# A hybrid encoder trunk in fp32: the second wave of group B's projections copied into output tiles, its rotary parts beside the latents' products, the latents in another order, the last squares of the MLP tied to a later place

## The chip, the core and the metric

The kernel runs on one core of a Trainium2 chip. The metric is the device time of one execution in microseconds (us). TensorE is called PE in the profile, VectorE DVE, ScalarE ACT, GpSimd POOL, SyncE SP.

## What is computed

Two layers over x of 1024 tokens by 1024 features, float32. Each layer has a projection of the normed x whose columns go to four groups of heads, the groups' attentions, one output projection with the residual, and an MLP with squared ReLU:

```python
for l in range(DEPTH):                       # DEPTH = 2
    h = rms_norm(x, norm1_g[l])
    proj = h @ w_in[l]
    (a_cq, a_ckv, a_kr, b_q, b_k, b_v, c_q, c_k, c_v, d_q, d_k, d_v) = jnp.split(proj, splits, axis=-1)
    y_a = mla_mixer(a_cq, a_ckv, a_kr, ...)  # latents: q = norm(cq) @ w_uq, k, v = norm(ckv) @ w_uk, w_uv
    y_b = diff_mixer(b_q, b_k, b_v, ...)     # q, k rotary; two softmaxes, w = p0 - lam * p1
    y_c = swa_mixer(c_q, c_k, c_v, ...)      # window of 128, sinks
    y_d = na_mixer(d_q, d_k, d_v, na_rpb[l]) # neighbourhood on the 64-wide grid, with a bias
    mix = jnp.concatenate([rms_norm(y_a, ..), y_b, rms_norm(y_c, ..), rms_norm(y_d, ..)], axis=-1)
    x = x + mix @ w_out[l]
    h = rms_norm(x, norm2_g[l])
    x = x + jnp.square(jax.nn.relu(h @ w_up[l])) @ w_down[l]
return rms_norm(x, final_norm_g)
```

Group A has 4 heads over latents of 192 (query) and 128 (key and value), B 4 heads of two 32-wide parts, C 4 query heads, D 4 heads.

## The kernel before

The products are made of fp32r parts: `split` (L195, L198) writes the rounded high half on ACT, then the low half as a difference (`tt`, L189), for weights on POOL (wh, wl). Each product is three passes, high by high (L221), low by high (L222) and high by low (L223) as `passes` orders them. x and all activations stand with features on the partitions and tokens along the free axis.

The program is written in the order of the stages, and a scheduler decides the order of each engine's instructions from it, with a few hints in the code: `high_priority` draws work forward, and `issue_after(ins)` keeps what is inside it behind the instruction named.

**Group B.** The projections of B come in two waves of six PSUM banks (`several`, WAVES): per wave a tile of q, of k and of v. When a wave is done, ACT copies each bank raw into a tile (L480): at both waves into `ptile`, the ring of tiles named p (six of them) that the softmax uses for its scores and probabilities. From the raw copy an evacuation (`ev`, from `evacs_b`, L423 to L427) makes q and k rotary (part<-p,tabc: the cosine part; twice part<-p,tabs: the sine parts with halves exchanged; an addition; the split; the stores into qb and kb) or turns v. The first wave's additions and low halves stand on DVE, the second wave's on POOL (`self.eng`). The turning of v (`to_values`) makes four transposes into a bank: the first wave's are put off (`self.due`, drained by `catch_up` in later steps of a projection), the second's are done at once, in a bank "tr".

Then `weave` mixes attn_b (scores sb, L856; minimum of each row nm, L858 on DVE; exponentials on ACT; transposes tr, L892; products pv) with a fill: `proj_latent` (the latents' projections, mm<-xh) and then `proj_d` (the projections of D).

**The latents.** attn_d and, beside it, proj_c and `latent_up` (L740) follow. The latter loads the normed factors (rq, rkv: spread over the partitions), the latents (latp: high and low; the key's and value's latent, and the query's of 128 and of 64 rows, the latter loaded twice each) and multiplies them with w_lat: values, keys, then the query's parts and the query's rotary part. rkv is loaded first, rq last. The bias of D's heads comes through the same SP queue.

**The MLP.** mlp_up works in 16 groups with a scheme of seven products for each two by two block; its results (ev) are rectified (`relu2`, L1254: max(u, 0) times the norm's factor, on DVE; the square on ACT), their differences made (`differ`), and stored into acts. mlp_down runs j = 0 to 3, each with operations 1, 2, 6, 7, 4, 5 and 3, and adds each block into x (x<-u, x<-p on DVE, L189), on which the reuse of the bank u waits. raw are weights with their sums, far the rounded activations' low halves. Since the last group of mlp_up ends when mlp_down already begins, its end is kept as `finish_up`: two functions, of which mlp_down calls the first in j = 0 after the first operation, behind `rounded` (the last rounding of its operands), the second in j = 1. The p blocks of j = 0 are tied behind `self.rectified`, the rectification written last.

## Time and profile before

| | |
|---|---|
| median of 3 runs | 2660.11 us (2659.59 to 2661.64) |
| the profiled execution | 2666.08 us |
| its span, first to last instruction | 2664.3 us |
| granted clock of PE, mean | .971 |
| busy: PE, DVE, ACT, POOL | 2529.8 (95%), 1950.1 (73%), 1442.6 (54%), 1127.8 (42%) us |
| DMA | 385.00 MB, mean 145 GB/s |

Busy times are sums over the whole span and say how full an engine is on average. What a change at one place is worth is read there: by windows (busy time of every engine in a stretch), by the waits of an engine in it (which engine's instruction came last before it went on) and by the timeline of one engine. A timeline's row joins equal instructions that follow each other; in brackets stands the idle time before it and what ended it. The clock is granted in parts of the full 2.4 GHz: 1.00 or .50 for a stretch, between them where it changes in a window.

### The profile page before, as it was taken

Reading aid. Unit: us, or ns where it says so; the run is one execution under the profiler, and the core shown is the slowest. Engines: PE = TensorE matmul, PEld = TensorE weight load, DVE = VectorE, ACT = ScalarE, POOL = GpSimd, SP = SyncE. Lnnn points to the kernel's source line nnn. Section 1 sums busy time; section 2 is a strip of 40 time slices with the busy share of each in tenths; the row PEclk is TensorE's granted clock in tenths of the full one; section 3 lists DMA queues with packets and bytes.
Section 4 is the critical chain, followed back from the end, with each engine's and each line's share of the span. In section 5 each row is a group of like instructions: output and inputs, shape, how many; then the busy total and the mean of one; then the engine's idle time right before and its main releaser. Section 6 shows DMA issues by size and latency. Waiting matters only on the chain.

```text
span 2664.3 us, 37498 instructions
## 1 busy us (share of the span) xinstructions
PE 2529.8 (95%) x12320; PEld 2105.1 (79%) x12320; DVE 1950.1 (73%) x3403; ACT 1442.6 (54%) x2612; POOL 1127.8 (42%) x800
## 2 busy tenths in 40 slices
PE   8899988999999998999999999889999999999998
PEld 7678877887788886888877788777877888878886
DVE  6677767784986668887568777677849866688876
ACT  4577756663644444444436777666735444444445
POOL 2465633211055554454425656332011555555554
PEclk9889998999999999999998999989999999999999
DMA  5634598331244456444245445963221544664431
GB/s 167 181 89 127 145 266 252 106 92 36 76 162 150 152 189 240 145 140 143 93 120 150 117 134 145 291 199 90 84 71 32 187 154 150 228 215 149 129 119 64
DMA packets 191539, 385.00 MB, mean 145 GB/s; under 512 B 23712, under 2 KB 34928, under 8 KB 191344
## 3 DMA queue, kind: packets, MB, share of 16 engines
q1 hardware_dynamic: 176976, 356.90, 44.2%
q10 hardware_dynamic: 14368, 25.70, 2.8%
q8 instruction: 98, 1.61, 0.3%
q14 instruction: 97, 0.79, 0.1%
HBM read 261.20 MB, written 121.32 MB: 144 GB/s over the span
## 4 chain that ended last, share of the span: by engine, by line
PE 73%; DVE 11%; DMA 7%; ACT 4%; issue 3%; POOL 1%; SPq 1%; DVEq 0%; POOLq 0%; ACTq 0%
PE u L221 8%; PE u L223 8%; PE u L222 8%; PE mm L221 5%; PE p L223 5%; PE p L221 5%; PE p L222 5%; PE mm L222 5%; PE mm L223 5%; PE sb L856 3%; DVE p L858 3%; PE tr L892 2%; DVE part L189 2%; ACT p L861 1%; PE pv L881 1%
## 5 line engine op out<-in xcount | busy, mean ns | idle before, releaser
L189 POOL TENSOR_TENSOR wl<-raw,wh 128x512 fp32r<-128x512 f32 x424 | 605.6, 1430 | 698.9 <-ACT wh L195 675.0
L195 ACT ACTIVATE wh<-raw 128x512 fp32r<-128x512 f32 x448 | 281.3, 629 | 578.3 <-PE u L222 311.4
L189 POOL TENSOR_TENSOR wl<-ws,wh 128x512 fp32r<-128x512 f32 (+1 forms) x120 | 151.1, 1261 | 451.1 <-ACT wh L195 444.2
L221 PE MATMUL u<-far,wh 128*128 128x512 f32 x768 | 301.1, 392 | 11.4 <-DVE x L189 9.2
L223 PE MATMUL u<-far,wl 128*128 128x512 f32 x768 | 300.9, 392 | 6.7 <-POOL wl L189 6.7
L222 PE MATMUL u<-far,wh 128*128 128x512 f32 x768 | 300.7, 392 | 0.0
L189 DVE TENSOR_TENSOR raw<-raw 128x512 f32<-128x512 f32 x256 | 224.9, 886 | 79.4 <-DMA raw<-in_w_up 43.1
L189 DVE TENSOR_TENSOR ptl<-tr,pth 128x512 fp32r<-128x512 f32 (+2 forms) x384 | 237.8, 628 | 60.5 <-ACT pth L195 59.4
L861 ACT ACTIVATE p<-p,nm 128x1024 f32<-128x1024 f32 x192 | 220.1, 1147 | 79.0 <-DVE nm L858 77.2
L195 ACT ACTIVATE pth<-tr 128x512 fp32r<-128x512 f32 (+2 forms) x384 | 206.0, 547 | 99.7 <-PE tr L892 63.6
L223 PE MATMUL p<-far,wl 128*128 128x512 f32 (+1 forms) x648 | 251.0, 387 | 4.0 <-DVE wl L189 4.0
L221 PE MATMUL p<-far,wh 128*128 128x512 f32 (+1 forms) x648 | 251.3, 388 | 0.0
L222 PE MATMUL p<-far,wh 128*128 128x512 f32 (+1 forms) x648 | 250.9, 387 | 0.0
L856 PE MATMUL sb<-stack 96*128 96x512 f32 x640 | 223.2, 430 | 13.9 <-DVE nm L858 12.9
L189 DVE TENSOR_TENSOR far<-act,far 128x512 fp32r<-128x512 f32 x224 | 206.1, 949 | 14.6 <-ACT far L195 14.6
L189 POOL TENSOR_TENSOR p<-p 128x1024 f32<-128x1024 f32 x64 | 154.8, 2419 | 106.3 <-ACT p L944 99.5
L221 PEld LDWEIGHTS u<-far,wh 128*128 128x128 f32 x768 | 145.1, 189 | 43.3 <-issue 10.0
L223 PEld LDWEIGHTS u<-far,wl 128*128 128x128 f32 x768 | 145.3, 189 | 37.9 <-POOL wl L189 7.8
L222 PEld LDWEIGHTS u<-far,wh 128*128 128x128 f32 x768 | 145.2, 189 | 31.0 <-DVE far L189 0.8
L221 PE MATMUL mm<-xh,wh 128*128 128x512 f32 x416 | 166.8, 401 | 1.8 <-DVE part L189 1.6
L892 PE MATMUL tr<-ident,p 128*128 128x128 f32 x1024 | 162.1, 280 | 6.3 <-DVE ptl L189 5.4
L858 DVE CUSTOM_DVE_ANT_0 p<-sb,zero 128x512 f32<-128x512 f32 x192 | 129.3, 685 | 49.5 <-PE sb L856 22.1
(255 smaller groups left out, 6150.7 us busy)
## 6 DMA issues: line engine op xcount, KB each, us to landing
act<-acts SPq DMA_DIRECT2D x224, 256.0 KB
raw<-in_w_up SPq DMA_DIRECT2D x128, 256.0 KB
acts<-ev SPq DMA_DIRECT2D x128, 256.0 KB
raw<-in_w_down SPq DMA_DIRECT2D x128, 256.0 KB
acts<-ev ACTq DMA_DIRECT2D x96, 256.0 KB
ws<-in_w_in SPq DMA_DIRECT2D x76, 256.0 KB
rz<-drows SPq DMA_DIRECT2D x40, 256.0 KB
stack<-kd SPq DMA_DIRECT2D x32, 256.0 KB
```

The costliest lines, as they stand in the source:

```text
L189: return (eng or self.nc.vector).tensor_tensor(out=out, in0=a, in1=b, op=op)
L195: self.rounded = nc.scalar.activation(hi, src, AF.Copy)
L221: mm(ps, w[0], x[0][:, sl], start=start, stop=False)
L222: mm(ps, w[0], x[1][:, sl], start=False, stop=False)
L223: mm(ps, w[1], x[0][:, sl], start=False, stop=stop)
L856: self.nc.tensor.matmul(ps, q[:, qt * P:(qt + 1) * P], k[:, sl], start=i == 0, stop=i == len(passes) - 1)
L858: self.nc.vector.tensor_tensor_reduce(out=p[:, sl], in0=ps, in1=self.zero[:, 0:1].bitcast(F).broadcast_to([P, 512]), scale=-scale, scalar= ...
L861: self.nc.scalar.activation(p, p, AF.Exp, bias=nm[:, 1:2], scale=-1.0, accum_out=z)
L881: nc.tensor.matmul(out, v[:, kt], lo[:, sl], start=False, stop=kt == 7)
L892: nc.tensor.transpose(t[:, k * 256 + i * P:k * 256 + (i + 1) * P], p[:, (j * 2 + k) * P:(j * 2 + k + 1) * P], self.ident)
```

## The change

Three parts, each in both layers. First, the second wave's raw copies go into output tiles (`ypair`, the tiles named y), and its evacuations are queued and done one by one, each ahead of a step of proj_latent; its values are turned like the first wave's. Second, latent_up loads both factors first and then the query's latents ahead of the others, and multiplies in another order: query rotary, query 0, key 0, both values, query 1, key 1. Third, the end of the last group of mlp_up is divided anew: in j = 0 only one rectification and one addition are left (`free`), and the squares, the other two rectifications, the differences and their stores (`rest`) stand in j = 1, tied behind the last addition of its first operation. `self.rectified` is thereby the rectification in `free`.

```diff
         def evacs_b(t):
             return [self.ev_rope(tabs, qb[:, t]), self.ev_rope(tabs, kb[:, t]),
-                    self.ev_plain(rb, self.to_values(vb[2 * t:2 * t + 2], "tr" if t else "mm"))]
+                    self.ev_plain(rb, self.to_values(vb[2 * t:2 * t + 2]))]
...
+                    second = deque()
+
+                    def beside(steps):
+                        for s in steps:
+                            if second:
+                                ev, n, src = second.popleft()
+                                ev(n, src)
+                            yield s
+
                     for t in range(2):
                         for ev, b in zip(evacs_b(t), banks):
-                            raw = self.ptile()
+                            raw = self.ypair() if t else self.ptile()
                             for n in range(2):
                                 sl = slice(n * 512, n * 512 + 512)
                                 nc.scalar.activation(raw[:, sl], b[n], AF.Copy)
-                                ev(n, raw[:, sl])
+                                if t:
+                                    second.append((ev, n, raw[:, sl]))
+                                else:
+                                    ev(n, raw[:, sl])
...
-                    fill = chain(self.proj_latent(l, one, xs, rb, tabs, lat, krd, rows), proj_d())
+                    fill = chain(beside(self.proj_latent(l, one, xs, rb, tabs, lat, krd, rows)), proj_d())
...
     def latent_up(self, l, lat, rows, qa, ka, va):
-        rkv = self.big_tile(F, "rkv")
-        kv = latent(2, P)
-        self.spread(rkv, rows[1])
-        q = [latent(0, P), latent(1, 64)]
-        rq = self.big_tile(F, "rq")
-        self.spread(rq, rows[0])
+        rq, rkv = self.big_tile(F, "rq"), self.big_tile(F, "rkv")
+        self.spread(rq, rows[0])
+        self.spread(rkv, rows[1])
+        parts = []
+        for i, r in ((0, P), (1, 64), (2, P)):
...
+        w0 = self.weights(d["w_lat"][l, 0])
+        yield from two([w0[0], both(w0[1])], parts[0:2], self.ev_rope(tabs, qr))
         plain = lambda r, dst: self.ev_plain(r, self.to_parts(dst))
+        yield from two([w0[2], both(w0[3])], parts[0:2], plain(rq, qn[:, 0]))
+        w1 = self.weights(d["w_lat"][l, 1])
+        yield from two(w1[2:3], parts[2:3], plain(rkv, kn[:, 0]))
         w2 = self.weights(d["w_lat"][l, 2])
         for t in range(2):
-            yield from two(w2[t:t + 1], [kv], self.ev_plain(rkv, self.to_values(va[2 * t:2 * t + 2])))
-        w1 = self.weights(d["w_lat"][l, 1])
-        for t in range(2):
-            yield from two(w1[2 + t:3 + t], [kv], plain(rkv, kn[:, t]))
-        yield from two([w1[0], both(w1[1])], q, plain(rq, qn[:, 1]))
-        w0 = self.weights(d["w_lat"][l, 0])
-        yield from two([w0[0], both(w0[1])], q, self.ev_rope(tabs, qr))
-        yield from two([w0[2], both(w0[3])], q, plain(rq, qn[:, 0]))
+            yield from two(w2[t:t + 1], parts[2:3], self.ev_plain(rkv, self.to_values(va[2 * t:2 * t + 2])))
+        yield from two([w1[0], both(w1[1])], parts[0:2], plain(rq, qn[:, 1]))
+        yield from two(w1[3:4], parts[2:3], plain(rkv, kn[:, 1]))
...
-            self.finish_up = [lambda: (done4(s), done3(s)), lambda: differ(s)]
+            def free():
+                s.b21 = tmp()
+                rectify(s.b21, s.u, 0)
+                self.tt(s.u2, s.p, s.u2, ALU.add)
+
+            def rest():
+                nc.scalar.activation(s.b21, s.b21, AF.Square)
+                keep(s.q, 2, s.b21)
+                relu2(s.u3, s.u3, 1)
+                keep(s.q, 3, s.u3)
+                relu2(s.u2, s.u2, 1)
+                differ(s)
+
+            self.finish_up = [free, rest]
...
-                        add(m, 0, u[m])
+                        added = add(m, 0, u[m])
...
                 if j == 1:
-                    self.finish_up[1]()
+                    with tc.issue_after(added.ins):
+                        self.finish_up[1]()
```

What it moves, in three places. The first is DVE where layer 0's attn_b begins: sb are the scores, nm their minima, part<-p the rotary products of the second wave's raw copies; both<-mm, the turning of the first wave's values, is the last row that the two have in common. Before:

```order
L189 TENSOR_TENSOR both<-mm,both 128x8x64 x2
L189 TENSOR_TENSOR part<-p,tabc 128x512
L189 TENSOR_TENSOR part<-p,tabs 64x512 x2
L189 TENSOR_TENSOR part<-p,tabc 128x512
L858 ISA p,nm<-sb,zero 128x512
L858 ISA nm 128x1
L189 TENSOR_TENSOR part<-p,tabs 64x512 x2
L858 ISA p,nm<-sb,zero,nm 128x512
L858 ISA nm 128x1
L858 ISA p,nm<-sb,zero 128x512
L858 ISA nm 128x1
```

Now:

```order
L189 TENSOR_TENSOR both<-mm,both 128x8x64 x2
L867 ISA p,nm<-sb,zero 128x512
L867 ISA nm 128x1
L867 ISA p,nm<-sb,zero,nm 128x512
L867 ISA nm 128x1
L867 ISA p,nm<-sb,zero 128x512
L867 ISA nm 128x1
L867 ISA p,nm<-sb,zero,nm 128x512
L867 ISA nm 128x1
L867 ISA p,nm<-sb,zero 128x512
L867 ISA nm 128x1
L867 ISA p,nm<-sb,zero,nm 128x512
```

Behind the sixth reduction the rotary products follow, read from y (part<-y,tabc and part<-y,tabs), a few at a time between the following reductions.

The second place is DVE at the MLP's passage in layer 0; ev are the results of the last group of mlp_up, far and raw belong to j = 0 of mlp_down. Before:

```order
L189 TENSOR_TENSOR ev<-p,ev 128x512
L189 TENSOR_TENSOR far<-act,far 128x512 x8
L1256 SCALAR_TENSOR_TENSOR ev<-ev,rb 128x512
L1256 SCALAR_TENSOR_TENSOR ev<-u,rb 128x512
L189 TENSOR_TENSOR ev<-p,ev 128x512
L189 TENSOR_TENSOR far<-act,far 128x512
L1256 SCALAR_TENSOR_TENSOR ev<-ev,rb 128x512
L189 TENSOR_TENSOR raw<-raw 128x512 x4
L189 TENSOR_TENSOR far<-act,far 128x512 x3
L189 TENSOR_TENSOR raw<-raw 128x512
L189 TENSOR_TENSOR far<-act,far 128x512
```

Now:

```order
L189 TENSOR_TENSOR ev<-p,ev 128x512
L189 TENSOR_TENSOR far<-act,far 128x512 x8
L1270 SCALAR_TENSOR_TENSOR ev<-u,rb 128x512
L189 TENSOR_TENSOR raw<-raw 128x512 x4
L189 TENSOR_TENSOR ev<-p,ev 128x512
L189 TENSOR_TENSOR raw<-raw 128x512
L189 TENSOR_TENSOR far<-act,far 128x512
L189 TENSOR_TENSOR raw<-raw 128x512
L189 TENSOR_TENSOR far<-act,far 128x512
L189 TENSOR_TENSOR raw<-raw 128x512
L189 TENSOR_TENSOR far<-act,far 128x512
```

Two rectifications of ev are gone from here, and so are the four differences (ev<-ev) that stood between the additions into x that follow. They stand in j = 1, behind the last addition of the first operation:

```order
L189 TENSOR_TENSOR x_7190<-u,x_7190 128x512
L1270 SCALAR_TENSOR_TENSOR ev<-ev,rb 128x512 x2
L189 TENSOR_TENSOR far<-act,far 128x512 x2
L189 TENSOR_TENSOR raw<-raw 128x512
L189 TENSOR_TENSOR x_7169<-p,x_7169 128x512
L189 TENSOR_TENSOR ev<-ev 128x512
L189 TENSOR_TENSOR raw<-raw 128x512
L189 TENSOR_TENSOR x_7176<-p,x_7176 128x512
L189 TENSOR_TENSOR ev<-ev 128x512 x3
L189 TENSOR_TENSOR x_7183<-p,x_7183 128x512
```

The third place is SP's queue at the latents of layer 0. Before:

```order
L160 DMA rz<-drows 64x1024
L160 DMA v<-vd 128x1024
L160 DMA latp<-lat 128x1024 x2
L160 DMA rkv<-drows 128x1024
L160 DMA latp<-lat 128x1024 x2
L160 DMA latp<-lat 64x1024 x4
L160 DMA rq<-drows 128x1024
L160 DMA ws<-in_w_out 128x256
L160 DMA stack<-kd 64x1024 x2
L160 DMA stack<-kc 64x1024
L160 DMA bias<-in_bias 128x768
```

Now:

```order
L160 DMA rz<-drows 64x1024
L160 DMA rq<-drows 128x1024
L160 DMA rkv<-drows 128x1024
L160 DMA latp<-lat 128x1024 x2
L160 DMA latp<-lat 64x1024 x4
L160 DMA latp<-lat 128x1024 x2
L160 DMA bias<-in_bias 128x768
L160 DMA stack<-kd 64x1024 x2
L160 DMA stack<-qd 64x1024
```

The loads of the latents stand in one piece, with both factors ahead of them, and they come ahead of more of attn_d's loads (stack).

## Rows read from the trace of the kernel before

**Rows 1.** The page: the chain's shares by engine, and the group of GpSimd's low halves.

```profile
PE 73%; DVE 11%; DMA 7%; ACT 4%; issue 3%; POOL 1%; SPq 1%; DVEq 0%; POOLq 0%; ACTq 0%
...
L189 POOL TENSOR_TENSOR wl<-raw,wh 128x512 fp32r<-128x512 f32 x424 | 605.6, 1430 | 698.9 <-ACT wh L195 675.0
```

**Rows 2.** Windows, us: stretch, length, busy PE, PEld, DVE, ACT, POOL, PEclk, DMA share, GB/s.

```profile
98.00:118.00 20.00, 13.45 (x40) 9.04 (x39) 19.20 (x41) 13.95 (x24) 14.78 (x9) 0.58 0.51 153
118.00:155.00 37.00, 36.66 (x210) 31.58 (x209) 30.16 (x68) 28.42 (x46) 20.45 (x13) 1.00 0.43 124
155.00:180.00 25.00, 23.17 (x94) 17.50 (x93) 20.94 (x54) 18.64 (x30) 18.23 (x16) 0.66 0.40 117
1418.00:1438.00 20.00, 14.28 (x47) 10.16 (x46) 18.89 (x42) 14.73 (x24) 14.12 (x9) 0.66 0.58 175
```

**Rows 3.** Timeline of VectorE from 83 to 92 us: start, us, instruction.

```profile
83.53 0.69 DVE L189 TENSOR_TENSOR part<-p,tabc 128x512 f32<-128x512 f32 x1 [17.63 <-ACT p L480]
84.24 2.42 DVE L189 TENSOR_TENSOR part<-p,tabs 64x512 f32<-64x512 f32 x2
86.69 0.69 DVE L189 TENSOR_TENSOR part<-p,tabc 128x512 f32<-128x512 f32 x1
...
88.57 3.46 DVE L189 TENSOR_TENSOR part<-p,tabs 64x512 f32<-64x512 f32 x2 [0.58 <-POOL part L189]
```

**Rows 4.** Waits of TensorE, 98 to 120 us: total, times, longest.

```profile
PE sb L856 <- DVE nm L858: 5.3, 2, 2.9
```

**Rows 5.** Waits of TensorE, 1000 to 1060 us.

```profile
PE u L221 <- DVE x L189: 9.2, 2, 7.6
...
PE u L223 <- POOL wl L189: 0.6, 1, 0.6
```

**Rows 6.** Timeline of TensorE from 1054 to 1060.5 us.

```profile
1055.43 0.77 PE L221 MATMUL u<-far,wh 128*128 128x512 f32 x1 [7.58 <-DVE x L189]
...
1060.24 0.40 PE L223 MATMUL u<-far,wl 128*128 128x512 f32 x1
```

**Rows 7.** Timeline of VectorE from 1008 to 1060 us.

```profile
1012.94 1.77 DVE L1256 SCALAR_TENSOR_TENSOR ev<-ev,rb 128x512 f32<-128x512 f32 x1
...
1016.43 0.68 DVE L1256 SCALAR_TENSOR_TENSOR ev<-ev,rb 128x512 f32<-128x512 f32 x1
...
1032.77 0.68 DVE L189 TENSOR_TENSOR ev<-ev 128x512 f32<-128x512 f32 x1
...
1040.64 3.48 DVE L189 TENSOR_TENSOR ev<-ev 128x512 f32<-128x512 f32 x2
...
1048.73 1.75 DVE L189 TENSOR_TENSOR ev<-ev 128x512 f32<-128x512 f32 x1
...
1054.61 1.87 DVE L189 TENSOR_TENSOR x<-u,x 128x512 f32<-128x512 f32 x3
```

**Rows 8.** Timeline of TensorE from 2345 to 2350 us.

```profile
2347.67 0.79 PE L223 MATMUL u<-far,wl 128*128 128x512 f32 x1 [6.04 <-POOL wl L189]
```

**Rows 9.** The chain, 2335 to 2350 us, in order of time: start, us, what.

```profile
2340.29 7.34 POOL wl L189
```

**Rows 10.** Windows at the MLP's passage and in j = 1, layer 0.

```profile
1050.00:1060.00 10.00, 4.57 (x11) 3.68 (x12) 9.48 (x16) 0.00 (x0) 0.00 (x0) 0.50 0.77 257
1110.00:1120.00 10.00, 10.00 (x46) 8.29 (x45) 10.00 (x12) 4.31 (x8) 5.55 (x4) 1.00 0.30 93
1125.00:1130.00 5.00, 5.00 (x24) 4.14 (x23) 2.54 (x4) 1.26 (x2) 2.16 (x3) 1.00 0.83 260
```

**Rows 11.** Waits of TensorE, 350 to 490 us.

```profile
PE sb L1026 <- DVE nb L1102: 4.0, 1, 4.0
...
PE mm L221 <- DMA latp<-lat: 2.2, 1, 2.2
```

**Rows 12.** Window of the latents' loads.

```profile
350.00:372.00 22.00, 18.82 (x106) 16.08 (x104) 10.35 (x28) 12.65 (x34) 6.80 (x4) 1.00 1.03 305
```

**Rows 13.** Waits of VectorE, 340 to 490 us.

```profile
DVE p L1102 <- DMA bias<-in_bias: 12.7, 3, 7.0
```

More of the change, by code (lines that the diff above doesn't have):

```diff
@@ L741, in latent_up @@
         nc, d = self.nc, self.d
-        def latent(i, r):
+        rq, rkv = self.big_tile(F, "rq"), self.big_tile(F, "rkv")
[3 more added lines that the diff above has]
+        for i, r in ((0, P), (1, 64), (2, P)):
             p = []
@@ L748, in latent @@
                 p.append(t)
-            return tuple(p)
-        rkv = self.big_tile(F, "rkv")
-        kv = latent(2, P)
-        self.spread(rkv, rows[1])
-        q = [latent(0, P), latent(1, 64)]
-        rq = self.big_tile(F, "rq")
-        self.spread(rq, rows[0])
+            parts.append(tuple(p))
         tabs = self.table("32", rq, nc.gpsimd)
@@ L1254, in relu2, with rectify @@
             def relu2(v, src, n):
+                rectify(v, src, n)
+                nc.scalar.activation(v, v, AF.Square)
+                return v
+            def rectify(v, src, n):
                 self.rectified = nc.vector.scalar_tensor_tensor(out=v, in0=src, scalar=0.0, in1=rb[:, N[n]],
                                                                 op0=ALU.max, op1=ALU.mult)
-                nc.scalar.activation(v, v, AF.Square)
-                return v
             def keep(q, o, v, eng=None):
@@ L1449, in add @@
                 o = self.x[m][:, N[n]]
-                self.tt(o, ps, o, ALU.add)
+                return self.tt(o, ps, o, ALU.add)
             for j in range(4):
```

## The prediction

> **What bounds the kernel now.** I read the page's chain first: 73% of the end is TensorE, 11% VectorE, 7% DMA, 4% ScalarE [rows 1]. TensorE is busy for 2529.8 of 2664.3 us, so all that an order without a new instruction can win lies in some 134 us of TensorE's idle time, and in matmuls that run at half clock behind an idle stretch. So I looked where the change moves something, by windows, and asked in each what TensorE waits for. Three places come out, each once per layer (layer 1 is layer 0 plus about 1318 us).
>
> The first is the start of group B's attention. From 98 to 118 us VectorE is busy for 19.20 of 20 us and TensorE for 13.45, at a granted clock of .58; in layer 1 it is 18.89 and 14.28, at .66 [rows 2]. The waits of TensorE there name the softmax's minimum on VectorE (nm) first, 5.3 us [rows 4]: VectorE is the bound of that stretch, and its rotary work of the second wave stands in the same queue as the softmax. From 118 to 155, TensorE is full (36.66 of 37) and VectorE has 6.84 us free; from 155 to 180 TensorE loses 1.83 us [rows 2].
>
> The second is the loading of the latents, 350 to 400 us, where the DMA engines are full (share 1.03, 305 GB/s) [rows 12]. TensorE waits 2.2 us for a latent tile and 4.0 us for a softmax [rows 11], and VectorE 12.7 us in all for the band's bias, which is loaded through the same queue [rows 13].
>
> The third is the passage from the MLP's up to its down products. In layer 0 TensorE waits 9.2 us for VectorE's additions into x, 7.6 of it at once [rows 5, 6], and VectorE has no free time before that. In layer 1 it waits 6.04 us for a low half (wl) of GpSimd [rows 8], which took 7.34 us [rows 9] where the mean of 424 is 1.43 [rows 1].
>
> **The change, part by part.** No engine gets an instruction more or fewer; everything is order, so no term is a duration by itself, only what a queue holds when somebody waits for it.
>
> *The MLP's passage, layer 0.* Ahead of the three additions x<-u at 1054.61 that TensorE waits for, VectorE ran two rectifications and four differences that now stand in the next quarter (j = 1): 1.77, .68, .68, 3.48 for two, and 1.75, in all 8.36 us [rows 7]. At the .68 of an undisturbed one six would cost 4.1 us; the rest was sharing with GpSimd, which may move to whoever comes next. So VectorE arrives 4.1 to 8.4 us earlier. TensorE can win the wait of 9.2 at most, and with it part of the slow matmuls behind it: from 1055.43 to 1060.24 eleven matmuls start in 4.81 us, with the granted clock of that window at .50, the level of 1.2 GHz [rows 6, 10]; at 2.4 GHz they would take half, so 2.4 us hang on the wait. I take **-6 us**, about the middle of 4.1 and 8.4; bounds -1 (the sharing comes back, and more) and -10 (8.4 and most of the 2.4).
>
> *The same in layer 1.* There TensorE waits for GpSimd's wl. VectorE's work that goes away stands partly before, partly behind that wl, and what kept GpSimd out, the row of raw and far operations with two operands in SBUF, stays. The later b21 rectification reads PSUM and may let GpSimd in, or not. Bounds 0 and -8 (6.04 and some 2 of slow matmuls); nearest to an unchanged row, I take **-2**.
>
> *The work put into j = 1.* Two rectifications, four differences, three squares and six stores land behind the first block's last addition of j = 1. VectorE is full there (10.00 of 10 us from 1110 to 1120) but TensorE lost nothing, and by 1125 to 1130 VectorE is busy for 2.54 of 5 only [rows 10]. Six times .68 is 4.1 us against those 2.5 us of free time, and what TensorE has in hand there no row shows: 0 to 3 us of delay per layer; **+1** for both. ScalarE, which gets the squares and two of the stores, is busy for 4.31 of 10 us there [rows 10], so they hide. The tensors stored are read in j = 3 only. Four of the stores stand in SP's queue, now behind j = 1's twelve loads of activations; while they wait for the differences, the loads of weights for the second half of the quarter wait behind them. If the cover is gone, the products of operation 6 in j = 1 are late by what is left of the 4.1.
>
> *The second wave beside the latents.* The copies by ScalarE stay, into output tiles; so the second wave holds no tile of the p ring, which the softmax uses. Of VectorE's rotary work, .69, 2.42, .69 and 3.46, together 7.26 us, was done from 83.5 to 92 us [rows 3], while TensorE was full with the wave's last products and the first latents. In the new order VectorE goes straight into six score reductions there, and those 7.26 us fall later. The second reduction can stand some 4 us earlier, since nothing of 3.46 us is ahead of it. The price has two ends: a loss of 7.26 per layer if they fall into VectorE's full stretch, a gain of up to 6.55 us (5.72 in layer 1), TensorE's idle time of it, if the softmax goes ahead and the rotary work moves to where TensorE has products. The only free VectorE time beside such products is the 6.84 us of 118 to 155, about what is moved. So I take **0** per layer, bounds -7 and +7. The two transposes of values that were done at once are now queued, at the same cost.
>
> *The latents in their old order.* First rq and rkv are loaded (1.05 MB), then all latent tiles, the query's first. The first product needs two tiles more (1.05 MB), its second half another two. At 305 GB/s [rows 12] 3.1 MB take 10.3 us, where before 1.05 MB (3.4 us) let the first product go. Against it: all loads stand together and earlier in SP's queue, ahead of head 1's bias, whereas rq came last before. The bounds per layer are +7 (10.3 - 3.4, in full) and -6 (the waits of 2.2 and 4.0 gone [rows 11]); in between, the nearest row is the wait of 2.2, a change of which is small: **0**. That the bias comes later falls to VectorE's waits for it, 12.7 us over three, of which TensorE felt at most 4.0.
>
> The sum: -6 - 2 + 1 + 0 + 0 = **-7 us** against the profiled execution of 2666.08, so 2659.1. That execution is 5.97 above the median of the runs, 2660.11, so in the terms of the runs the forecast is **2653.0 us**. The bounds of the three terms of the MLP alone reach from -18 to +5.
>
> **A rule against it.** GpSimd's low half took 7.34 us in layer 1 while VectorE ran operations on SBUF back to back, and a pair of VectorE's rotary operations 3.46 us [rows 3, 9]. The Trainium skill, "SBUF — State Buffer", section "SBUF: two separate sides", says that VectorE's operations with two SBUF operands and GpSimd's share a port pair that is an exclusive lock: who starts first has it for the whole instruction, the other stops. The trace agrees with the stop, by 7.34 against 1.43. In both orders 14 operations on SBUF alone stand ahead of the first addition into x; by that rule they can keep GpSimd out in layer 0 as in layer 1, and the sum would be -2 in place of -7.
>
> **The rivals.**
> - *GpSimd is locked out at both passages.* Layer 0 exchanges the wait of 9.2 for one like layer 1's 6.04, with the same slow matmuls behind; that is -3; layer 1 gives 0, j = 1 +1: -2, or **2658 us**. For it: the 7.34 us. Against it: in layer 0 TensorE waits for wl only 0.6 us [rows 5].
> - *The interleaving fills TensorE.* The stretches of 98 to 118 lose 6.55 and 5.72 us; if the softmax's head start carries through, both layers win that: 2653 - 12.3, about **2640 us**. For it: VectorE full and named by the waits [rows 2, 4]. Against it: the work is the same and comes in a full stretch.
> - *Slower: VectorE's early time is lost.* The 7.26 us of rotary work that TensorE covered from 83 to 92 now fall where VectorE sets the pace, in both layers: 2653 + 14.5, about **2667 us**. It decides above 6.2 us per layer ((5.3 + 7)/2). For it: VectorE is idle for 17.63 us before 83.5 [rows 3] and full behind 98. Against it: its 6.84 us free from 118 on.
> - *The latents stand at their loads.* At +6 per layer: 2653 + 12, **2665 us**. For it: full DMA engines; against it: the earlier issue.
> - That the change doesn't do what it says is excluded by the order of the instructions: the rotary work, the loads and the differences stand where the diff says.
>
> **How the numbers follow.** A measurement of this kernel can tell 0.2% (5.3 us) from no change, so faster is below 2654.8, slower above 2665.4. Forecast .36 (.33 faster, .03 same; by itself 2647 to 2658), filling .20 (faster), early time lost .17 (slower), lock .15 (same), loads .12 (.09 same, .03 slower): faster .53, same .27, slower .20. The range goes from the filling's 2641 to 2666, by the lost time's edge; left out are the ends on both sides, some .2.
>
> **What would show it.** Right: TensorE's wait for x from 1000 to 1060 us falls from 9.2 to about 3, the windows of 98 to 118 keep about 13.5 us of TensorE, and no wait for latp above 5 us appears. Wrong: a wait for wl of 6 us in both layers (the lock), TensorE above 17 us from 98 to 118 (filling) or a longer stretch of its half clock (lost time), a wait for latp near 7 us (loads).

## The result, and the profile after

The changed kernel takes 2672.47 us (median of 6 runs, 2668.89 to 2677.04) against 2658.05 for the kernel before in 6 runs beside it: a ratio of 1.0056, 95% interval 1.0041 to 1.0071. It is **slower by some 15 us**, where 7 us less were forecast. It lies outside the range, on the side and some 5 us beyond the size of the third rival (VectorE's early time lost, 2667).

A word on the reference of all that follows. The kernel before ran 71 times in five sets beside the others, 2652.3 to 2671.7 with medians of 2658 to 2661, but its two profiled executions took 2666.08 and 2667.54. The profile that the prediction read is thus an execution 6 us above the median. Where one profile of the attention in its old order is needed, I therefore also use that of experiment e3 (below), which leaves the attention as it was and whose profiled execution, 2652.6, is its own median.

Windows of the changed kernel at the start of layer 0's attention, in the columns of [rows 2]:

```profile
80.00:92.00 12.00, 12.00 (x54) 9.88 (x53) 2.21 (x7) 4.09 (x8) 2.59 (x2) 1.00 0.96 241
98.00:118.00 20.00, 13.59 (x62) 10.53 (x60) 15.63 (x31) 11.25 (x18) 13.47 (x7) 0.91 0.30 90
118.00:155.00 37.00, 34.54 (x178) 29.11 (x179) 33.59 (x69) 23.99 (x40) 26.46 (x18) 0.92 0.50 134
155.00:180.00 25.00, 19.25 (x90) 14.94 (x89) 19.58 (x54) 19.26 (x32) 16.91 (x15) 0.79 0.49 153
```

and of the kernel before in the first of them:

```profile
80.00:92.00 12.00, 12.00 (x54) 9.90 (x53) 7.82 (x8) 4.72 (x9) 6.05 (x4) 1.00 1.03 228
```

From 80 to 92 us VectorE is now busy for 2.21 us where it was for 7.82: the rotary work is gone from there. From 98 to 118 it is busy for 15.63 of 20 (19.20 before). TensorE's busy time is almost the same there, 13.59 against 13.45, but it holds 62 matmuls instead of 40 [rows 2], at a granted clock of .91 instead of .58: for a while the changed kernel is ahead. The two later windows take that back: TensorE loses 2.46 and 5.75 us, where it lost .34 and 1.83, and makes 178 and 90 matmuls, where it made 210 and 94.

The timeline of VectorE there, start, duration, instruction, and in brackets the idle time before it:

```profile
86.33 0.69 DVE L867 CUSTOM_DVE_ANT_0 p<-sb,zero 128x512 f32<-128x512 f32 x1 [20.77 <-PE sb L865]
...
87.50 0.75 DVE L867 CUSTOM_DVE_ANT_0 p<-sb,zero,nm 128x512 f32<-128x512 f32 x1 [0.46 <-PE sb L865]
...
91.86 0.75 DVE L867 CUSTOM_DVE_ANT_0 p<-sb,zero,nm 128x512 f32<-128x512 f32 x1 [3.00 <-PE sb L865]
...
96.19 0.68 DVE L189 TENSOR_TENSOR part<-y,tabc 128x512 f32<-128x512 f32 x1
...
99.00 3.81 DVE L189 TENSOR_TENSOR part<-y,tabs 64x512 f32<-64x512 f32 x2
...
111.74 0.69 DVE L867 CUSTOM_DVE_ANT_0 p<-sb,zero 128x512 f32<-128x512 f32 x1 [2.65 <-PE sb L865]
```

and the second reduction in the kernel before:

```profile
92.07 0.75 DVE L858 CUSTOM_DVE_ANT_0 p<-sb,zero,nm 128x512 f32<-128x512 f32 x1
```

The first reduction follows 20.77 us of idle time. The second comes at 87.50, so the head start of some 4 us that I expected is there; it is 7.1 us at the sixth reduction and 6.5 at the twelfth. Then it is lost. The first rotary part of the second wave comes at 96.19, and its sine pair, 3.81 us (1.38 for another such pair at 116.50), stands between two halves of a softmax, from 99.00 to 102.8. And at 111.74 VectorE waits 2.65 us for scores: between its scores at 103.66 and 111.20 TensorE made 21 matmuls of the fill. By the 20th score 31 of the fill's weight tiles (three matmuls each) are done, where 24 were before.

What that does later, two windows show, from 64 to 88 us behind the first score, of the kernel before and of the changed one:

```profile
150.10:174.10 24.00, 22.40 (x96) 17.49 (x95) 20.07 (x46) 16.95 (x26) 19.72 (x15) 0.72 0.50 131
```

```profile
149.90:173.90 24.00, 16.83 (x75) 12.85 (x74) 19.93 (x51) 17.36 (x29) 18.16 (x12) 0.76 0.71 206
```

Up to there the two have made 275 and 276 matmuls; in these 24 us they make 96 and 75. The last of the latents' 48 tiles begins 59.6 us behind the first score in the changed kernel, 66.9 before, and the next tile of the fill only at 90.9 and 93.6. In between TensorE has nothing but the softmax's work, which in the changed kernel is behind: at 64 us 33 of its transposes are done, where 48 were before.

TensorE's waits from 85 to 209 us, from 1410 to 1534 (layer 1), and in the kernel before from 86 to 203:

```profile
PE sb L865 <- DVE nm L867: 7.0, 6, 3.3
PE tr L901 <- POOL p L189: 3.6, 1, 3.6
PE mm L221 <- DVE sq L712: 2.6, 1, 2.6
```

```profile
PE sb L865 <- DVE nm L867: 7.4, 5, 2.8
PE tr L901 <- POOL p L189: 6.2, 1, 6.2
```

```profile
PE sb L856 <- DVE nm L858: 5.8, 4, 2.9
```

The wait for the minimum (nm) rose from 5.8 to 7.0 us (in layer 1 from 4.6 to 7.4), and there is a new one: transposes that wait for GpSimd's sum of the two softmaxes (p), 3.6 and 6.2 us. GpSimd's timeline in layer 1 shows what stood ahead of it:

```profile
1488.27 2.34 POOL L189 TENSOR_TENSOR tabc<-tabc,rb 128x1024 f32<-128x1024 f32 x1 [2.17 <-DMA tabc<-in_c]
...
1490.97 2.34 POOL L189 TENSOR_TENSOR tabs<-tabs,rb 128x1024 f32<-128x1024 f32 x1
1493.27 2.34 POOL L189 TENSOR_TENSOR p<-p 128x1024 f32<-128x1024 f32 x1
```

Since the latents' products end earlier, the tables that follow them (two of 2.34 us, the first after a wait for its load) come ahead of the p that TensorE wants: behind seven of these sums of attn_b, where it was eight before.

At the MLP's passage, TensorE's waits in layer 0 (1000 to 1060 us) and in layer 1 (2310 to 2390):

```profile
PE u L223 <- POOL wl L189: 6.0, 1, 6.0
```

```profile
PE u L223 <- POOL wl L189: 6.6, 1, 6.6
```

The wait for x of 9.2 us [rows 5] is gone in layer 0, and a wait for wl of 6.0 us stands in its place, as in layer 1. That is the rival of the lock, to the tenth. GpSimd's row at that place and VectorE's queue beside it:

```profile
1028.55 11.16 POOL L189 TENSOR_TENSOR wl<-raw,wh 128x512 fp32r<-128x512 f32 x3 [4.72 <-ACT wh L195]
```

```profile
1030.91 1.28 DVE L189 TENSOR_TENSOR far<-act,far 128x512 fp32r<-128x512 f32 x2
...
1033.92 1.29 DVE L189 TENSOR_TENSOR far<-act,far 128x512 fp32r<-128x512 f32 x2
1035.12 0.69 DVE L189 TENSOR_TENSOR x<-u,x 128x512 f32<-128x512 f32 x1
```

GpSimd's three low halves take 11.16 us instead of some 4 (three times the mean of 1.43 [rows 1]), the first of them 7.77. VectorE goes through raw and far without a gap, and TensorE goes on at 1036.38, behind the first operation since then that reads PSUM (x<-u at 1035.12).

To compare stages of different kernels I take them from TensorE's instructions: stage B is from the first score of attn_b to the first of attn_d, stage D from there to the first of the next attention, "37 scores" from the first to the 37th matmul of scores in B (the latents' products lie in it), "tiles" are the weight tiles of the fill's products done when D begins (of 208 per layer, each three matmuls), "passage" is the time from the 257th to the 369th first pass of a far product. Layer 0 / layer 1, in us, each from one profiled execution:

| kernel | run, us | 37 scores | stage B | stage D | tiles | passage |
|---|---|---|---|---|---|---|
| before | 2666.1 | 71.7 / 70.1 | 247.2 / 244.6 | 147.8 / 152.2 | 184 / 184 | 89.4 / 85.4 |
| changed | 2671.0 | 77.8 / 75.2 | 254.8 / 257.5 | 152.3 / 142.4 | 192 / 192 | 84.0 / 84.4 |
| e0 before, again | 2667.5 | 71.5 / 70.1 | 246.1 / 244.8 | 145.2 / 152.5 | 184 / 184 | 89.8 / 89.2 |
| e1 second wave | 2684.9 | 79.7 / 81.3 | 256.3 / 257.1 | 155.4 / 144.4 | 192 / 191 | 89.9 / 89.6 |
| e2 latents | 2642.9 | 72.2 / 71.1 | 244.5 / 244.1 | 141.8 / 137.4 | 184 / 184 | 89.2 / 88.9 |
| e3 squares | 2652.6 | 71.6 / 70.1 | 244.7 / 244.6 | 144.6 / 146.4 | 184 / 184 | 85.3 / 84.5 |
| e4 = e1 + e2 | 2686.1 | 79.6 / 75.9 | 256.3 / 249.0 | 149.5 / 157.5 | 192 / 176 | 89.5 / 89.3 |
| e5 = e2 + e3 | 2648.6 | 71.7 / 72.2 | 247.2 / 245.8 | 148.5 / 144.5 | 184 / 185 | 84.9 / 84.7 |
| e6 tiles, late turn | 2675.1 | 75.7 / 75.0 | 251.6 / 251.1 | 151.9 / 148.5 | 183 / 183 | 89.9 / 89.3 |
| e7 query early | 2672.8 | 73.1 / 72.7 | 250.1 / 242.4 | 147.8 / 157.4 | 192 / 176 | 89.9 / 90.2 |
| e8 tiles alone | 2665.9 | 73.5 / 71.3 | 248.2 / 247.7 | 148.1 / 148.0 | 184 / 185 | 89.6 / 90.3 |
| e9 late turn alone | 2675.5 | 75.4 / 73.2 | 252.7 / 244.2 | 146.7 / 164.4 | 184 / 176 | 85.4 / 89.2 |
| e10 late, turned in tr | 2686.8 | 76.2 / 80.6 | 256.3 / 265.1 | 139.5 / 153.0 | 192 / 192 | 89.6 / 89.4 |
| e11 late, in p | 2677.5 | 81.0 / 83.3 | 246.7 / 249.0 | 153.2 / 156.8 | 176 / 176 | 88.8 / 89.9 |
| e12 changed, query early | 2661.8 | 73.8 / 72.6 | 250.8 / 240.7 | 148.0 / 156.6 | 192 / 176 | 85.7 / 84.8 |
| e13 changed, more fill | 2656.4 | 76.5 / 81.6 | 251.9 / 254.5 | 145.9 / 141.5 | 184 / 187 | 84.8 / 85.8 |

Three executions with the attention in one and the same order (before, e0, e3) differ by 2.5 us in a stage B and by 6 in a stage D, so smaller differences between single entries say nothing.

### The profile page after: what moved, and what is told of

Same layout as the page of the kernel before. It is cut to its first block, busy times and chain, and to the rows that moved or that the text cites. A ratio compares the mean times of both kernels' runs of the same rounds, so it can differ in the third digit from the quotient of the medians.

```text
span 2669.2 us, 37508 instructions
## 1 busy us (share of the span) xinstructions
PE 2521.7 (94%) x12320; PEld 2095.1 (78%) x12320; DVE 1936.8 (73%) x3403; ACT 1443.8 (54%) x2612; POOL 1129.7 (42%) x800
## 5 line engine op out<-in xcount | busy, mean ns | idle before, releaser
L865 PE MATMUL sb<-stack 96*128 96x512 f32 x640 | 216.6, 418 | 18.6 <-DVE nm L867 17.2
L189 DVE TENSOR_TENSOR far<-act,far 128x512 fp32r<-128x512 f32 x224 | 200.5, 925 | 14.6 <-ACT far L195 14.6
L223 PEld LDWEIGHTS u<-far,wl 128*128 128x128 f32 x768 | 144.9, 189 | 43.6 <-POOL wl L189 13.5
```

Of the source, the lines that this page charges most:

```text
L189: return (eng or self.nc.vector).tensor_tensor(out=out, in0=a, in1=b, op=op)
L223: mm(ps, w[1], x[0][:, sl], start=False, stop=stop)
L865: self.nc.tensor.matmul(ps, q[:, qt * P:(qt + 1) * P], k[:, sl], start=i == 0, stop=i == len(passes) - 1)
```

## The experiments

**The three parts by themselves.** e1, e2 and e3 are the kernel before with the first, second and third block of the diff alone. e0 is the kernel before.

e1, the second wave: 

> The kernel before with the first part of the change alone (second wave's raw copies in output tiles, its rotary parts one per step beside the latents' products). Theory A (VectorE's early rotary work, 7.26 us per layer, falls where VectorE sets the pace of the softmax): slower than before by 14 to 25 us, TensorE 7 us or more later at the 28th score of attn_b in both layers. Theory B (the loss is in the latents' loads, the rotary work costs nothing): within 4 us of before. Theory C (the wave and the latents only cost together): within 5 us here and in the next run.

Measured: 2682.5 us, ratio 1.0077 (1.0060 to 1.0094), some +20. Counted from the first score, the 28th is reached 8.2 and 10.3 us later than in the kernel before. That is theory A's number, and B falls. But A is not yet shown: copies, the turning of the values and the order of the fill changed with it.

e2, the latents: 

> The kernel before with the second part alone (both factors and the query's latents loaded first, products in the other order). Theory A: no loss, -6 to 0 us against before. Theory B: slower by 10 to 15 us, with TensorE waiting for a latent tile more than 5 us per layer.

Measured: 2646.1 us, ratio 0.9945 (0.9930 to 0.9961), some -15: better than either theory said. TensorE still waits for a latent, 4.2 us, once:

```profile
PE mm L221 <- DMA latp<-lat: 4.2, 1, 4.2
```

What went is seen in the other waits of layer 0's stage D. These are e3's from 332 to 476.6 us, whose attention is as before (the first line stands word for word in the kernel before as well):

```profile
PE sb L1026 <- DVE nb L1133: 5.7, 2, 4.5
PE sb L1026 <- DVE nb L1102: 5.1, 1, 5.1
```

and this is all that e2 has left of them, from 331.4 to 473.4:

```profile
PE sb L1023 <- DVE nb L1130: 0.5, 2, 0.3
```

nb are the minima of the softmaxes of groups D and C. So 10.8 us of waits became .5, against which the waits for latp rose from .7 us to 5.4 (the 4.2 and one of 1.2). In layer 1 other waits went; TensorE's idle time in the stage falls from 18.9 to 14.3 us. Windows of the stage for e2 in both layers, for e3, and for e5, which loads the latents as e2 does:

```profile
331.40:473.40 142.00, 128.48 (x715) 108.61 (x714) 103.66 (x265) 95.43 (x246) 57.52 (x48) 0.94 0.87 256
1639.60:1777.00 137.40, 123.14 (x712) 104.15 (x711) 105.03 (x266) 97.79 (x251) 58.06 (x49) 0.96 0.87 264
```

```profile
332.00:476.60 144.60, 124.93 (x697) 108.32 (x695) 101.39 (x258) 94.30 (x243) 55.51 (x47) 0.92 0.84 246
1642.50:1788.80 146.30, 127.41 (x717) 109.67 (x716) 106.34 (x267) 97.45 (x247) 57.98 (x49) 0.93 0.84 249
```

```profile
331.40:480.00 148.60, 128.41 (x715) 108.20 (x715) 104.38 (x265) 95.69 (x247) 58.30 (x49) 0.94 0.86 245
1643.50:1788.00 144.50, 125.86 (x714) 105.97 (x712) 109.34 (x268) 97.88 (x246) 58.45 (x49) 0.95 0.85 252
```

Time by rate is 35.6 to 36.4 MB in all six: the stage moves about the same bytes, so e2's higher rate (256 and 264 GB/s) is the shorter stage in other words. It does not show that loads issued in one piece run faster; e5, with the same piece, has 245 and 252, and the changed kernel has 237 in layer 0.

e3, the squares: 

> The kernel before with the third part alone (the last group's squares and differences in j = 1). By the forecast's term: faster by 7 us (3 to 12), TensorE's wait for x at the MLP's passage of layer 0 below 4 us. By the lock rival: faster by 2 us at most, and a wait for wl of about 6 us in both layers.

Measured: 2652.63 us, ratio 0.9974 (0.9959 to 0.9990), -7 with -3 to -11 for its interval. The size is the forecast's, the mechanism the rival's: no wait for x is left and the wait for wl is 6.7 us in both layers.

```profile
PE u L223 <- POOL wl L189: 6.7, 1, 6.7
```

The passage takes 84.0 to 85.8 us in all ten passages of the five kernels with this part, and 88.8 to 90.3 in twenty of the twenty-two without it (85.4 in the other two): some 4.6 us per layer between the middles. The two short ones, layer 1 of the profile that I read and layer 0 of e9, have a wait for wl of 6.0 us without the change; the other twenty have one for x of 9.1 or 9.2.

e0: 

> The kernel before, unchanged, for a second profile. If the first profiled execution (2666.1 us, 8 above the median) was an unlucky one at the MLP's passage, the waits for x and wl there are shorter here (under 9 and 6 us); if not, they stand again and the difference lies in the attention.

Measured: 2667.54 us. Layer 1 has TensorE's wait for x of 9.2 us here, not the wait for wl:

```profile
PE u L221 <- DVE x L189: 9.2, 2, 7.6
```

So neither was the first profile unlucky at the passage (it was lucky there in layer 1) nor does the passage explain the 6 us; most of them are in the attention, where e3 in the same order is 2 to 6 us shorter per layer.

**Do the parts add up?** +20, -15 and -7 make -2, and the whole is +15. Left out of the whole one at a time (e5 and e4 below), the second wave costs some 28 us, more than alone, and the squares win some 13. The changed kernel without the second part was not run.

e4, the first and second: 

> The kernel before with the first and second part, without the third. If the parts' times add up (+22 for the first, -13 for the second): slower than before by 9 us. If the first part takes away what the second wins (the latents' products come earlier in group D's attention than their loads, as the order of the first part puts them at its 22nd score instead of its 34th): slower by 18 to 24 us.

Measured: 2685.7 us, ratio 1.0098 (1.0084 to 1.0112), +26. Beside the second wave's part the latents' part is worth nothing: the interval overlaps that of e1 alone. In its layer 0, and in both layers of the changed kernel, the first latents' product now stands behind 22 scores of attn_d, not 34 (layer 0) or 30 (layer 1). Where that happens in the changed kernel, TensorE's waits in stage D of layer 0 are

```profile
PE mm L221 <- DMA latp<-lat: 3.4, 1, 3.4
...
PE mm L222 <- DMA latp<-lat: 1.8, 1, 1.8
...
PE mm L780 <- DMA latp<-lat: 1.4, 2, 1.1
```

6.6 us in all for latp, against 5.4 in e2, so these waits alone don't carry it. In layer 1 of e4 the scheduler put 34 there and left 176 tiles; stage D is 157.5 long. What it is in the order that takes the second part's gain away I can point to, but not isolate.

e5, the second and third: 

> The kernel before with the second and third part, without the first. If the parts add up: faster than before by 18 to 22 us, 2638 to 2642. If the second part's gain hung on the order of the rest: between 2643 and 2655.

Measured: 2644.84 us, ratio 0.9943 (0.9931 to 0.9955), -15. It is faster than both kernels, but the parts don't add up to -22 here either; the second expectation holds. The passage is short in both layers, so the loss is in the attention: layer 0 has e2's counts (34 scores, 184 tiles), and is longer by 2.7 and 6.7 us in B and D all the same. Part of that is scatter: e2's profiled execution is the fastest of its five runs, e5's the slowest of its six.

**What in the second wave's part costs?** In e6 every piece is evacuated at once, from y and with the late turn:

```diff
-                                if t:
-                                    second.append((ev, n, raw[:, sl]))
-                                else:
-                                    ev(n, raw[:, sl])
+                                ev(n, raw[:, sl])
```

> The kernel before with the second wave's copies in output tiles and its values turned like the first wave's, but every rotary part at once, as before. Theory A (the postponed rotary work costs): within 5 us of before. Theory D (the tiles and the softmax running ahead in the free ring cost): slower by 12 us or more, like the whole first part.

Measured: 2675.1 us, ratio 1.0061 (1.0048 to 1.0073), +16. With the rotary work where it was, most of the cost is there. Theory A alone falls.

In e7 only the query's rotary parts (those that stood from 83 to 92 us) are done at once:

```diff
-                        for ev, b in zip(evacs_b(t), banks):
+                        for e, (ev, b) in enumerate(zip(evacs_b(t), banks)):
...
-                                if t:
+                                if t and e:
```

> The first part with the query's rotary parts at once and only the key's and the values' beside the latents. Theory A: between the two, slower than before by 6 to 14 us. Theory D: slower by 18 us or more. If only the last postponed pieces cost, it stands with the whole first part as well.

Measured: 2672.58 us, ratio 1.0053 (1.0037 to 1.0068), +14. The total is at the edge of A's bound. The stretch that A speaks of is clear, though: the first 37 scores take 73.1 and 72.7 us against e1's 79.7 and 81.3, with 334 matmuls in them instead of 328. What is lost stands elsewhere, in a stage D of 157.4 in layer 1 that begins with 176 tiles done.

e8 takes the tiles alone: `raw = self.ypair() if t else self.ptile()` in the kernel before, all else as it was. 

> Output tiles alone: the second wave's copies in y, its rotary parts and the turning of its values at once as before. Theory D (the tiles cost): slower by 12 us or more. Theory E (the postponed turning of the values, through the bank that the projections use, costs): within 6 us of before. Theory F (nothing in the first wave costs by itself; each edit lays the scheduler's order of the attention anew): between the two, with the loss where no edit stands, in group D's attention.

Measured: 2666.19 us, ratio 1.0019 (1.0005 to 1.0032), +5. The tiles cost little; theory D falls.

e9 takes the late turn alone: `self.to_values(vb[2 * t:2 * t + 2])` in evacs_b, copies in p. 

> The turning of the second wave's values alone postponed, copies in p tiles and rotary parts as before. Theory D: within 6 us of before. Theory E: slower by 12 us or more, like the run with tiles and postponed turning.

Measured: 2677.25 us, ratio 1.0061 (1.0040 to 1.0083), +16. So two postponed turns of values, in another bank, cost as much as e6: it is this that e6 paid for. At the 12th score 8 tiles of the fill are done, not 16, and at the 20th 16, not 24: the fill comes behind the scores. TensorE waits more for the softmax in the first 37 scores, 7.2 us in six waits (5.3 in two before):

```profile
PE sb L856 <- DVE nm L858: 7.2, 6, 2.4
```

e10 is the whole first part with the values turned in tr: `self.to_values(vb[2 * t:2 * t + 2], "tr" if t else "mm")` in e1. 

> The whole first part but the values turned in the bank tr when their turn comes. Theory A (postponed rotary work) and theory D: slower than before by 18 to 24 us, as the whole first part. Theory E: slower by 5 to 10 us.

Measured: 2686.55 us, ratio 1.0097 (1.0074 to 1.0120), +26. Beside postponed rotary work the projections' bank costs nothing (the intervals of e1 and e10 overlap); theory E doesn't explain e1. e8 and e10 differ only in the postponement, with y and tr in both, and stand at +5 and +26: some 21 us for it. Between e6 and e1, which differ by the same edit of the rotary parts with the late turn in both, it is some 4. So the two postponements don't add.

e11 postpones the rotary parts, with the copies in p and the turn in tr. 

> The rotary parts beside the latents' products, but the copies in p tiles and the values turned in tr: the postponement alone. Theory A: slower by 14 us or more, and by more still where the p ring is held. Theory D and E: within 8 us of before.

Measured: 2677.45 us, ratio 1.0058 (1.0039 to 1.0078), +15, as A said, though the copies now also hold p tiles longer, which this run doesn't separate. The first 37 scores take 81.0 and 83.3 us, the longest of all. The windows of them in layer 0, here and in e12 (below):

```profile
86.20:167.30 81.10, 71.89 (x332) 59.04 (x332) 64.86 (x137) 48.99 (x80) 50.09 (x33) 0.85 0.47 132
```

```profile
86.00:159.80 73.80, 66.70 (x334) 54.70 (x333) 61.53 (x135) 49.76 (x81) 44.28 (x30) 0.91 0.55 156
```

Nearly the same matmuls (332 and 334) and 3.3 us more of VectorE, but 7.3 us more time.

**The cause in the changed kernel itself.** e12 is the changed kernel with e7's edit. 

> The changed kernel with the query's rotary parts of the second wave at once, everything else as changed. Theory A: the first 37 scores of group B's attention take 71 to 74 us per layer as before, not the changed kernel's 75 to 78; the kernel stands 8 to 14 us below the changed one, 2658 to 2665, still above the kernel with the second and third part alone (2645). If the early VectorE time had no part in it: within 4 us of the changed kernel.

Measured: 2662.88 us, ratio to before 1.0007 (0.9994 to 1.0019), 9.6 below the changed kernel's 2672.47, as A expected. The first 37 scores take 73.8 and 72.6 us, inside the expected 71 to 74. The fill comes as early as in the changed kernel (32 tiles by the 20th score), and 64 us behind the first score 296 matmuls are made in either layer, where the changed kernel has 275 and 289: up to there the rotary work's place is the main difference. The bracket has a flaw: in layer 1 the scheduler also left 176 tiles in place of 192, so stage B's 16.8 us less there stand against 14.2 more in D.

e13 is the changed kernel with `RB = (6, 8)` in place of (7, 8). 

> The changed kernel with 8 steps of fill for every 6 of group B's attention in the program's order, not 7, which lets the scheduler leave 184 and 187 of the 208 weight tiles' products done when group D's attention begins (the kernel before: 184; the changed one: 192). If products done early in group B's attention cost there and give nothing back in group D's, where the loads set the end: group B's stage 4 to 6 us per layer shorter, group D's not longer, the kernel 6 to 12 us below the changed one. If only VectorE's early time counts: the same time as the changed kernel, within 4 us.

Measured: 2660.21 us, ratio to before 0.9998 (0.9984 to 1.0013), 12.3 below the changed kernel. Stage B is shorter by 2.9 and 3.0 us (I had said 4 to 6), and stage D is not longer but shorter by 6.4 and .9. The 37 scores stay at 76.5 and 81.6: VectorE's early time is as lost as before, and yet the kernel is level with the one before (though not with e5, which lacks only the second wave's part, and stands 15 below). The first product of the latents stands behind 34 and 28 scores of attn_d again, so part of the 12.3 may be the second part's gain coming back; the run doesn't separate the two. But the order around the second wave counts for as much as theory A.

## Why the prediction was wrong

**The second wave, taken at 0 with bounds of -7 and +7 per layer: the step that failed.** It costs 20 us alone, 10 per layer. Beside the other two parts it costs some 28 (2672.47 against e5's 2644.84). What failed is that VectorE's 6.84 free us from 118 to 155 were set against the 7.26 that move. They do not lie in one piece behind the softmax's work; a moved pair ran for 3.81 us between two reductions. Against e3 the changed kernel is longer by 6.2 and 5.1 us in the first 37 scores. The query's pieces done at once bring it back, by 6.6 and 8.6 us in e7 against e1 and by 4.0 and 2.6 in e12: this is the third rival. It was right on the place; the price, 2.6 to 8.6 us per layer, lies around its 7.26. Its sum 2653 + 14.5 came near the result partly by luck, since what follows was not in it.

The other part of the loss I had not on the list. The rotary work and the turn are ahead of the fill's products in the program, and moving them changes where the scheduler puts those. The softmax's head start, which I had as the price's better end, came true (7.1 us at the sixth reduction) and went into products of the fill, which then ran out: 75 matmuls instead of 96 in the 24 us behind. In the changed kernel 192 tiles are done when attn_d begins, before 184; those eight tiles are 24 matmuls, some 5.3 us at the 45 in 10 us of the windows further below. Stage B is 10.1 and 12.9 us longer than in e3, stage D 7.7 longer and 4.0 shorter. e13 edits just the fill and wins 12.3 us with the early time still lost; e9 loses 16 us with the rotary work in place. "At the same cost", which I wrote of the two turned transposes, holds for TensorE and VectorE's durations and was wrong for the order.

**The latents, taken at 0 with -6 to +7 per layer.** Alone they gain 15 us, 7 per layer, slightly beyond the better end. Here the price of 10.3 us for 3.1 MB was set against the wrong event. The first product's wait is 4.2 us, as the rows let one expect, and the waits that went are others: of the view in [rows 11] I took the 4.0 and the 2.2 and left out the largest, 5.7 us for the softmax of group C, so that the bound of -6 was too small. In the changed kernel that gain is missing: stages B and D together are 17.8 and 8.9 us longer than e3's (the rest of its execution is some 8 shorter). The latents now come behind 22 scores; that this is the cause isn't shown, since layer 1 of the changed kernel, with 22 as well, has a stage D of 142.4 us against e3's 146.4.

**The MLP's passage, -6, -2 and +1: the sum right by luck, the mechanism wrong.** e3 measured -7. But in place of VectorE's arrival it was the lock's rival that came true in both layers: VectorE reaches x<-u earlier, and TensorE then stands for wl. The measured gain is some 4.6 us per passage, of which 2.5 to 3.2 are the difference of the two waits. My -2 for layer 1 came from a profile in which layer 1 had the wait for wl already; e0 has 9.2 there. The lock's rival had the wait right and the price wrong (2 us at most), for the same reason. The rule of the Trainium skill ("SBUF — State Buffer", "SBUF: two separate sides") speaks of one instruction that keeps the other engine out for its whole length. The trace agrees that GpSimd stops, but for eleven of VectorE's instructions in a row: its low half took 7.77 us, and TensorE, which waited for it, went on 1.26 us behind the start of VectorE's next operation on PSUM. The work in j = 1 cost nothing: TensorE is busy for 10.00 of 10 us in the windows behind it,

```profile
1110.00:1120.00 10.00, 10.00 (x45) 8.28 (x45) 10.00 (x12) 4.22 (x7) 4.90 (x4) 1.00 0.39 115
1120.00:1130.00 10.00, 10.00 (x45) 8.26 (x44) 10.00 (x12) 5.79 (x10) 6.39 (x4) 1.00 0.51 158
```

so +1 was nearly right, with 0.

**The chances.** Slower had .20, and the likeliest slower rival named one half of the mechanism; its 2667 even lay outside the range, which ended at 2666. The weight was wrong for a reason that a reader can use: a term of 0 between -7 and +7 in two layers is not the likeliest case, it is no knowledge. VectorE stood at 19.20 of 20 us where the work was to go, and at 17.63 us idle where it was taken from; that row spoke for a loss. The signs named for a right forecast misled too: TensorE kept its 13.5 us from 98 to 118 and no wait for latp passed 5 us, but 13.59 us held 62 matmuls where 13.45 had held 40. Compare counts and clock beside busy time.

What stays open: how the loss divides between VectorE's early time and the place of the fill, since e12 and e13 each bring back some 10 to 12 us and each moves more of the order than what it tests; why the second part's gain disappears beside the first (e4), beyond the 22 scores, and which of the fill's places in B is good. Each edit moves the scheduler's order in stage D of layer 1 too, where no edit stands, and stages of 137 to 164 us came out of that.

## What to carry to other kernels

Work that fills an engine's idle time ahead of a stretch that this engine bounds is free where it stands; before moving it "beside" something, look for its idle time in the row that it leaves and in the row that it goes to, not in the average of the stretch. Where a scheduler makes the order, price an edit by the order of everything around it: count how much of the fill is done at each border of a stage, because what moves there can cost more than the instructions that were edited. And test the parts alone and without one another: here the best kernel was the second and third part without the first, 2644.84 us (ratio 0.9943), or the latents alone, 2646.1 (0.9945).

## What the runs showed of the hardware

The MLP's passage has two outcomes, and the same queues produce both. In layer 0 of the kernel before, VectorE and GpSimd took turns from 1018 to 1029 us: five of VectorE's operations took 1.77 to 1.79 us instead of .68 while four low halves took 1.66 to 1.85; VectorE came late, and TensorE waited 9.2 us for x. In layer 1 of the same execution none of VectorE's operations was slowed there, one low half took 7.34 us, and TensorE waited 6.04 us for wl. Without the third part the first outcome stands in twenty of 22 passages; with some 8 us of VectorE's work taken away, the second stands in all ten, at 6.0 to 6.7 us, and about half of what VectorE wins is left.

And a higher rate of the DMA engines in a stage need not be a gain of theirs: at about the same bytes (35.6 to 36.4 MB) stage D ran at 246 and 249 GB/s in e3, at 256 and 264 in e2, and at 245 and 252 in e5, whose loads of the latents stand in one piece as e2's do.
